# A convolution mixer's input projection: pairs of output tiles by seven half-size products, weight sums on GpSimd, some low weight parts by adding transfers

## The chip, the core and the metric

The kernel runs on one core of a Trainium2 chip. The core has a matrix engine (TensorE; PE in the profile, its weight loads PEld), a vector engine (VectorE, DVE), an activation engine (ScalarE, ACT), a general engine (GpSimd, POOL) and a queue engine that starts transfers (SyncE, SP), all with their own instruction streams that run in order and wait on semaphores. The metric is the device time of one execution in microseconds, median of the runs.

## The reference, cut to what matters

A trunk of four layers (mLSTM, short convolution, dilated attention, pooling) is run for 512 prompt tokens and 8 sample tokens that share all weights. The change is in layer 1:

```python
def shortconv_mixer(h, w_in, conv_w, w_out, buf):
    u = h @ w_in                       # 520 x 1024 by 1024 x 8192
    bg, cg, xb, z = jnp.split(u, 4, axis=-1)
    cx = cg * xb
    ...
    cpad = jnp.concatenate([buf.astype(cx.dtype), cx], axis=1)
    y = conv_w[0] * cpad[:, 0:T]
    for j in range(1, CONV_W):
        y = y + conv_w[j] * cpad[:, j:j + T]
    out = (bg * y * jax.nn.silu(z)) @ w_out
    return out, cpad[:, -(CONV_W - 1):]
```

All data are float32, and the products must come out at about float32 accuracy.

## The kernel before, in words

Activations lie with features on the 128 partitions and the 520 tokens along the free axis; a layer's input is 8 such tiles (1024 features). A weight tile is 128 x 1024: the 128 output features of one tile of the result, for 8 chunks of 128 input features. Every float32 operand is used as two float32r parts, hi = the rounded value and lo = the rest, and a product is hi·hi + hi·lo + lo·hi. `mm6` (L193) does this for one chunk: 3 products, each in two parts of 256 and 264 tokens, so 6 matmuls. `proj` (L213) makes one tile of the result from 8 chunks, 48 matmuls.

Weights come in the order that `plan` (L39) lists. `weights` (L181) is called when a tile is needed; it runs `cast` four tiles ahead and `fetch` six ahead: a load on SP (L165), the hi part by ACT (`wh`, L175) and the lo part by DVE (`wl`, L177, the load minus wh).

`conv` (L782) is layer 1's mixer. Its input projection has 64 weight tiles `w_b`. For each of 16 blocks j it takes four of them: 32+j (xb), 16+j (cg), j (bg) and 48+j (z). cx = cg·xb (L799), the taps of the convolution are one ACT instruction (L807) and four DVE ones (L810 to L813), POOL copies the last columns of cx out as state (L803, L804), and bg·y·silu(z) is made and split by `gated` (L517: L525, L528, L530) while the next block runs. `work` in `finish_norm` (L307) makes the normalised input tiles and their parts between the projections, from the `tick` that `proj` calls after every second chunk. The output projection `w_bo` follows (`out_proj`, L345). PSUM has two tiles of 1024 columns (`ps`) and four of 512 (`ax`).

Nothing moves instructions after the code has been written: each engine's order is the order of the calls.

Of the kernel before, what the change touches and what calls it, by code (L numbers as in the profile page):

```python
# [14 lines left out]
P = 128  # L15
# [8 lines left out]
H = 8  # L24
# [13 lines left out]

def plan():  # L39

    out = []

    def end(i, name, halves, begun=False):
        cs = range(2 if halves else 1)
        out.extend((name, j, c) if halves else (name, j) for c in cs for j in range(2) if c or not begun)
        out.extend((name, j, c) if halves else (name, j) for j in range(2, KD) for c in cs)
        for j in range(KD):
            if j % 4 == 0:
                out.append(("w_pe", i, j // 4))
# [12 lines left out]
    end(2, "w_co", False)
    for g in range(4):
        for n, (u, i) in enumerate(POOLED):
            if g and n == 2:
                out.extend(("w_grp", g - 1, i) for i in range(2))
            out.append(("w_d", 16 * u + 4 * g + i))
    out.extend(("w_do", j, 0) for j in range(2))
    out.extend(("w_grp", 3, i) for i in range(2))
    end(3, "w_do", True, True)  # L70
    return out

# [41 lines left out]
class Net:  # L114
    def __init__(self, ctx, tc, d):
# [5 lines left out]
        self.wp = pool("w", bufs=3)  # L121
# [7 lines left out]
        self.gate, self.finish = Gate(0.5), None  # L129
        self.wkeys, self.wf, self.wc = plan(), {}, {}  # L130
        self.wpos = self.ndma = self.ncast = 0
# [28 lines left out]

    def fetch(self, upto):
        while self.ndma < min(upto, len(self.wkeys)):
            key = self.wkeys[self.ndma]
            wf = self.wp.tile([P, 1024], F32, tag="wf", name=self.nm("wf"))
            self.nc.sync.dma_start(wf, self.d[key[0]][key[1:]])  # L165
            self.wf[self.ndma] = wf
            self.ndma += 1

    def cast(self, upto):
        nc = self.nc  # L170
        while self.ncast < min(upto, len(self.wkeys)):
            self.fetch(self.ncast + 1)
            wf = self.wf.pop(self.ncast)
            wh = self.wp.tile([P, 1024], F32R, tag="wh", name=self.nm("wh"), bufs=4)
            nc.scalar.activation(wh, wf, AF.Copy)  # L175
            wl = self.wp.tile([P, 1024], F32R, tag="wl", name=self.nm("wl"), bufs=4)
            nc.vector.tensor_sub(wl, wf, wh.bitcast(F32))  # L177
            self.wc[self.ncast] = (wh, wl)
            self.ncast += 1

    def weights(self, *key, ahead=4):  # L181
        i = self.wpos
        assert self.wkeys[i] == key, (self.wkeys[i], key)
        self.wpos += 1
        self.cast(i + ahead)
        self.fetch(i + 2 + ahead)
        return self.wc.pop(i)
# [5 lines left out]
    def mm6(self, ps, w, c, a, start, stop, m=P):  # L193
# [8 lines left out]
        for j in range(2):  # L202
            mm(out[j], wl, a[0][:, PARTS[j]], start=False, stop=stop)  # L203

# [8 lines left out]
    def proj(self, name, *idx, a):  # L213
# [5 lines left out]
        for c in range(0, n, 8):  # L219
            w = self.weights(name, *idx, *([c // 8] if n > 8 else []))  # L220
            for k in range(8):
                self.mm6(ps, w, k * P, a[c + k], c + k == 0, c + k == n - 1)
                if k % 2:
                    self.tick()
        return ps[:, BASE : BASE + T]

    def proj_pair(self, name, a, n):

        ps = self.psum(), self.psum()
        for c in range(0, n, 8):  # L230
            w = []
            for lo, hi in ((0, 7), (7, 8)) if c + 8 == n else ((0, 8),):
                for j in range(2):
                    if not lo:
                        w.append(self.weights(name, j, *([c // 8] if n > 8 else []), ahead=4 - j))
# [7 lines left out]
    def need(self, a, i):  # L243

        while len(a) <= i:
# [54 lines left out]
    def finish_norm(self, hs, g0, wait, idle, pace):  # L300
# [6 lines left out]
        def work():  # L307
# [14 lines left out]
            for _ in range(idle):  # L322
                yield
            new = []
# [18 lines left out]


    def out_proj(self, name, y, i, begun=None):  # L345
# [7 lines left out]
        for j in range(KD):  # L353
# [6 lines left out]
            xs.append(self.split(self.x[j]))  # L360
        return xs

    def embed(self, i, xs):
# [24 lines left out]
        self.finish_norm(hs, g0, 3, *((4, 4), (2, 3), (0, 0))[i])  # L388
# [393 lines left out]
    def conv(self, h, lay):  # L782
        nc, d, tc = self.nc, self.d, self.tc
        self.streams = [self.norm, self.gate]
        y = []
        ex = lay.enter_context(tc.tile_pool(name="cvy", bufs=16))
        with ExitStack() as st:
            mp = st.enter_context(tc.tile_pool(name="cv", bufs=1))
            sin = mp.tile([P, 16, 2, NS], F32, name="cv_in")
# [4 lines left out]
            for j in range(16):  # L794
# [8 lines left out]
                nc.gpsimd.tensor_copy(po[:, j], cx[:, NP - 2 : NP])  # L803
                nc.gpsimd.tensor_copy(so[:, j, 1], cx[:, NP:T])  # L804
                w0, w1, w2 = (self.col(C_CW + 16 * t + j) for t in range(3))
                yc = self.act()
                nc.scalar.activation(yc, cx, AF.Copy, scale=w2)  # L807
                ps = self.proj("w_b", j, a=h)
                stt = nc.vector.scalar_tensor_tensor
                stt(yc[:, 1:NP], cx[:, 0 : NP - 1], w1, yc[:, 1:NP], ALU.mult, ALU.add)  # L810
                stt(yc[:, 2:NP], cx[:, 0 : NP - 2], w0, yc[:, 2:NP], ALU.mult, ALU.add)
                stt(yc[:, NP:T], sin[:, j, 1], w1, yc[:, NP:T], ALU.mult, ALU.add)
                stt(yc[:, NP:T], sin[:, j, 0], w0, yc[:, NP:T], ALU.mult, ALU.add)  # L813
                nc.vector.tensor_mul(yc, self.ready(ps), yc)
# [524 lines left out]
```

## Time and profile before

| | us |
|---|---|
| median of 3 runs | 2192.8 |
| range of the runs | 2190.49 to 2194.71 |
| the profiled execution, its own time | 2191.75 |
| its span in the trace | 2190.0 |
| busy in the span: PE, DVE, ACT, POOL | 2170.4, 1336.6, 784.0, 226.8 |

A busy time is the union of an engine's instructions. Matmuls overlap in the pipeline, so one lasts some 285 ns by the trace and a new one starts about every 120 ns; what a matmul costs is read from a stretch of time and the matmuls in it. The convolution's input projection is the stretch from 606 to 975 us, its output projection the one from 975 to 1060 us.

### The profile page before, as it was taken

What the parts mean: (1) busy time and instruction counts of PE and PEld (TensorE: products, weight loads), DVE (VectorE), ACT (ScalarE), POOL (GpSimd) and SP (SyncE); (2) the same over time, 40 slices, a digit from 0 to 9 for tenths busy, and PEclk for the clock granted to TensorE, in tenths of its full rate; (3) what the DMA queues carried; (4) which work ended last, traced back from release to release, by engine and by line L of the source; (5) the groups of instructions that cost most, each with busy time, mean ns of one, the idle gap of its engine ahead of it and who ended that gap; (6) DMA issues with size and microseconds to landing.
All of it is one profiled execution on the core that took longest, in us unless ns stands there. A gap on an engine that the chain in (4) does not pass through costs nothing.

```text
span 2190.0 us, 42581 instructions
## 1 busy us (share of the span) xinstructions
PE 2170.4 (99%) x17788; PEld 2154.2 (98%) x17788; DVE 1336.6 (61%) x2984; ACT 784.0 (36%) x1286; POOL 226.8 (10%) x338
## 2 busy tenths in 40 slices
PE   9999999999999999999999999999999999999998
PEld 8999999999999999999999999999999999999998
DVE  7677676653575344333467877787777466676434
ACT  6444444432442222222333323333335343222233
POOL 1101110100000000000014232232220000000000
PEclk9999999999999999999999999999999999999999
DMA  4643544333232322233233645554545233323421
GB/s 151 203 163 139 184 168 150 98 97 97 90 97 87 97 89 95 92 105 95 83 103 127 187 168 179 172 181 155 184 161 194 87 106 97 97 88 97 124 88 51
DMA packets 104643, 275.17 MB, mean 126 GB/s; under 512 B 33316, under 2 KB 37668, under 8 KB 102404
## 3 DMA queue, kind: packets, MB, share of 16 engines
q1 hardware_dynamic: 104308, 272.41, 38.3%
q8 instruction: 139, 2.28, 0.4%
q14 instruction: 52, 0.43, 0.1%
q10 hardware_dynamic: 144, 0.06, 0.0%
HBM read 249.61 MB, written 22.82 MB: 124 GB/s over the span
## 4 chain that ended last, share of the span: by engine, by line
PE 91%; DVE 3%; ACT 1%; POOL 1%; issue 0%; DMA 0%; SPq 0%; POOLq 0%; DVEq 0%; ACTq 0%
PE ps L199 27%; PE ps L201 27%; PE ps L203 27%; PE ax L925 1%; PE ax L998 1%; PE ax L201 1%; PE ax L203 1%; PE ax L199 1%; PE ax L969 1%; PE ax L654 1%; PE ax L673 1%; DVE wl L177 1%; DVE a L329 0%; POOL a L877 0%; PE ax L936 0%
## 5 line engine op out<-in xcount | busy, mean ns | idle before, releaser
L199 PE MATMUL ps<-hi,wh 128*128 128x256 f32 (+1 forms) x5280 | 1086.3, 287 | 2.1 <-DVE a L278 1.6
L201 PE MATMUL ps<-lo,wh 128*128 128x256 f32 (+1 forms) x5280 | 1062.9, 283 | 0.1
L203 PE MATMUL ps<-hi,wl 128*128 128x256 f32 (+1 forms) x5280 | 1063.1, 283 | 0.0
L199 PEld LDWEIGHTS ps<-hi,wh 128*128 128x128 f32 x5280 | 822.3, 189 | 7.6 <-issue 2.5
L201 PEld LDWEIGHTS ps<-lo,wh 128*128 128x128 f32 x5280 | 819.3, 188 | 0.3 <-DVE lo L530 0.3
L203 PEld LDWEIGHTS ps<-hi,wl 128*128 128x128 f32 x5280 | 818.3, 188 | 0.0
L177 DVE TENSOR_TENSOR wl<-wf,wh 128x1024 fp32r<-128x1024 f32 x344 | 429.2, 1249 | 397.1 <-ACT wh L175 395.5
L175 ACT ACTIVATE wh<-wf 128x1024 fp32r<-128x1024 f32 x344 | 361.0, 1051 | 253.2 <-issue 201.7
L271 ACT ACTIVATE a<-ps 128x520 f32<-128x520 f32 x94 | 56.3, 599 | 247.7 <-PE ps L203 243.5
L876 POOL TENSOR_TENSOR a<-a,a 32x520 f32<-32x520 f32 x48 | 74.0, 1542 | 386.2 <-DVE a L278 199.6
L359 DVE TENSOR_TENSOR x<-ps,x 128x520 f32<-128x520 f32 x32 | 22.4, 699 | 103.4 <-PE ps L203 103.3
L278 DVE TENSOR_TENSOR a<-ps,a 128x520 f32<-128x520 f32 x95 | 65.9, 694 | 25.9 <-PE ps L203 22.5
L282 ACT ACTIVATE a<-a 128x520 f32<-128x520 f32 x43 | 27.5, 639 | 150.2 <-DVE a L278 150.0
L259 ACT ACTIVATE hi<-x 128x520 fp32r<-128x520 f32 x32 | 20.5, 639 | 164.6 <-DVE x L359 164.6
L877 POOL TENSOR_TENSOR a<-a,a 32x520 f32<-32x520 f32 x48 | 66.4, 1384 | 124.8 <-DVE a L875 88.7
L902 ACT ACTIVATE S<-S,nmx 128x128 f32<-128x128 f32 (+1 forms) x96 | 40.0, 417 | 76.1 <-DVE nmx L899 76.1
L252 DVE CUSTOM_DVE_ANT_0 kc<-kc,qb 128x128 f32<-128x128 f32 (+1 forms) x192 | 56.8, 350 | 12.5 <-DMA kc<-kc 12.5
L252 DVE CUSTOM_DVE_ANT_0 vc<-vc,pb 128x128 f32<-128x128 f32 (+1 forms) x192 | 61.6, 379 | 0.0
L880 DVE TENSOR_TENSOR a<-a,a 32x520 f32<-32x520 f32 x48 | 37.2, 776 | 17.3 <-POOL a L877 17.3
L260 DVE TENSOR_TENSOR lo<-a,hi 128x520 fp32r<-128x520 f32 x40 | 28.0, 699 | 31.3 <-ACT hi L259 31.3
L732 DVE SCALAR_TENSOR_TENSOR Ci<-kqb,wv,Ci 128x128 f32<-128x128 f32 x128 | 37.1, 346 | 12.2 <-DMA kqb<-scr_kq 10.1
L528 ACT ACTIVATE hi<-a 128x520 fp32r<-128x520 f32 x40 | 25.4, 635 | 50.6 <-DVE a L525 50.6
(272 smaller groups left out, 1759.7 us busy)
## 6 DMA issues: line engine op xcount, KB each, us to landing
wf<-w_c SPq DMA_DIRECT2D x80, 512.0 KB
wf<-w_a SPq DMA_DIRECT2D x64, 512.0 KB
wf<-w_b SPq DMA_DIRECT2D x64, 512.0 KB
wf<-w_pg SPq DMA_DIRECT2D x32, 512.0 KB
wf<-w_d SPq DMA_DIRECT2D x32, 512.0 KB
pb<-scr_p SPq DMA_DIRECT2D x8, 1292.0 KB
Ci<-C_in SPq DMA_DIRECT2D x16, 512.0 KB
kqb<-scr_kq SPq DMA_DIRECT2D x8, 1024.0 KB
```

Source lines behind the costliest of these rows:

```text
L175: nc.scalar.activation(wh, wf, AF.Copy)
L177: nc.vector.tensor_sub(wl, wf, wh.bitcast(F32))
L199: mm(out[j], wh, a[0][:, PARTS[j]], start=start, stop=False)
L201: mm(out[j], wh, a[1][:, PARTS[j]], start=False, stop=False)
L203: mm(out[j], wl, a[0][:, PARTS[j]], start=False, stop=stop)
L252: self.nc.vector.tensor_tensor_reduce(junk, a, b, 1.0, 0.0, ALU.mult, ALU.add, out)
L271: nc.scalar.activation(dst[:, :T], ps, func, scale=scale)
L278: nc.vector.tensor_mul(dst[:, :T], ps, self.r)
L876: nc.gpsimd.tensor_mul(b[:32], t[:32], cs[0])
L877: nc.gpsimd.tensor_mul(a[:32], a[:32], cs[1])
L880: nc.vector.tensor_add(t[:32], a[:32], b[:32])
L902: nc.scalar.activation(blk, blk, AF.Exp, bias=nmx[:, i : i + 1], scale=SCALE, accum_out=l[:, i : i + 1])
```

## The change

The first three blocks (NPLAIN) stay as they were. From block 3 on, the block's weight tiles are taken in two pairs, first (32+j, 16+j), then (j, 48+j), and each pair is one call of `seven`. It sees the product as two by two by two: two output tiles (w1, w2), two halves of the 1024 inputs (a, b: 512 columns of a weight tile each) and two halves of 260 tokens. Seven products of half size, in place of eight, make the two tiles. The weight operands are w1a, w1b, w2a' (in place: w1a − w2a), w2b and three sums s1, s2, s4. They are multiplied with input halves (11, 21, 22) and sums of those (T1 to T4). Each product is 4 chunks of 3 matmuls with 260 columns. The order on PE is: w1a·11, s2·T2, s1·T1, w1b·21, then the s4·22 of the pair before (`flush`), w2a'·T3, w2b·T4. After some of them ACT (L376, L384) or DVE (L379, L388, L392, and L371 behind the late product) add the results up.

The sums of weights are four GpSimd instructions a pair (L276 to L279), and the sums of the inputs 16 instructions of 260 columns, made once (`summed`). The parts hi and lo of s1, s2 and s4 are made by ACT and DVE (`hs`, `ls`, 512 columns). For the first tile of every w_b and w_bo item (the single tiles of blocks 0 to 2 and of w_bo too) the lo part is no longer a DVE subtraction: ACT writes −hi into it (L257), and a transfer that GpSimd issues adds the weight from memory onto it (L259). The two other parts of the work of a block are run when a pair's last product is there: `first` (cx and the taps) inside the second pair, `second` (silu and bg·y) inside the next block's first pair. The parts of y are made at the end, four of them in the last pair and the rest as the output projection asks for them.

When a step is written is now set by a list, `due`: it gives each load, split, sum and part a time on a clock in which a plain tile costs 5.76 and a pair 10.08, and `pump`, called after every matmul group, writes all that is due. Four loads can be held in place of three. The descriptor memory of GpSimd's transfers is set to 1024 bytes.

```diff
+NPLAIN = 3
+HALF = T // 2
+FBUFS, HBUFS, SBUFS = 4, 4, 4
+MOVED = ("w_b", "w_bo")
...
+        else:
+            ld, ld2 = sorted(slots["wf"])[:2]
+            one = at(max(ld, ld2, t - 12.8), i, "sum")
+            h1 = at(max(ld, take("wh", t + 5.76), t - 14.4), i, "high")
+            h2 = at(max(ld2, take("wh", t + 10.08), one + 4), i, "high2")
+            low1 = at(h1 + 1.3 if it.moved else max(h1 + 1.3, one + 3), i, "low")
+            low2 = at(max(h2 + 1.3, one + 3), i, "low2")
+            at(take("wf", max(low1, one + 5.8)) - 0.01, i, "load")
+            at(take("wf", low2) - 0.01, i, "load2")
+            for n, need, until in (("2", t - 7.2, t + 2.88), ("1", t - 5.7, t + 4.32), ("4", t - 1.4, t + 17.3)):
+                h = at(max(take("hs", until), need, one + 3), i, "high" + "s" + n)
+                at(h + 0.6, i, "lows" + n)
...
+        def high(k, tag, n=1024, pool=None):
+            t["h" + k] = new(tag, n, pool)
+            nc.scalar.activation(t["h" + k], t["w" + k], AF.Copy)
+
+        def low(k, tag, n=1024, pool=None):
+            t["l" + k] = new(tag, n, pool)
+            if k == "1" and it.moved:
+                nc.scalar.activation(t["l1"], f(t["h1"]), AF.Copy, scale=-1.0)
+                key = it.keys[0]
+                nc.gpsimd.dma_start(t["l1"], self.d[key[0]][key[1:]], accum_op=ALU.add)
+                return
+            nc.vector.tensor_sub(t["l" + k], t["w" + k], f(t["h" + k]))
...
+        elif op == "sum":
+            w1, w2 = t["w1"], t["w2"]
+            s1, s2, s4 = (self.act()[:, :512] for _ in range(3))
+            nc.gpsimd.tensor_add(s1, w2[:, a], w2[:, b])
+            sub(w2[:, a], w1[:, a], w2[:, a])
+            sub(s2, s1, w1[:, a])
+            sub(s4, w1[:, b], s2)
...
+    def seven(self, keys, B, dst, done):
...
+        def product(out, w, name, start):
+            for k in range(4):
+                c = slice(k * P, (k + 1) * P)
+                hi, lo = B[name][k]
+                go = {} if start else {"skip_group_check": True}
+                mm(out, w[0][:, c], hi, start=start and k == 0, stop=False, **go)
+                mm(out, w[0][:, c], lo, start=False, stop=False, **go)
+                mm(out, w[1][:, c], hi, start=False, stop=k == 3, **go)
...
+        def last():
+            product(r5, part("s4"), "22", False)
+            add(dst[0][:, HALF:], r5, u2)
+            done()
+            step()
+
+        product(r1, part("1", a), "11", True)
+        nc.scalar.activation(s1, r1, AF.Copy)
+        step()
+        product(r6, part("s2"), "T2", True)
+        add(u2, r6, s1)
+        step()
+        product(r5, part("s1"), "T1", True)
+        step()
+        product(r1, part("1", b), "21", False)
+        nc.scalar.activation(dst[0][:, :HALF], r1, AF.Copy)
+        step()
+        self.flush()
+        product(r6, part("2", a), "T3", False)
+        add(u3, r6, s1)
+        step()
+        product(r4, part("2", b), "T4", True)
...
+                def first():
+                    nc.vector.tensor_mul(cx, cx, xb)
+                    c.extend(taps(j, cx))
+                    conv(j, cx, *c)
+
+                def second():
+                    nc.scalar.activation(z, z, AF.Silu)
+                    nc.vector.tensor_mul(c[0], bg, c[0])
+                    self.gate.gens.append(times(c[0], z))
+
+                self.seven((("w_b", 32 + j), ("w_b", 16 + j)), self.sums, (xb, cx), first)
...
+                    self.seven((("w_b", j), ("w_b", 48 + j)), self.sums, (bg, z), second)
...
-    nc = bacc.Bacc("TRN2", target_bir_lowering=False, num_devices=1)
+    nc = bacc.Bacc("TRN2", target_bir_lowering=False, num_devices=1, dynamic_dma_scratch_size=1024)
```

On PE, before, one chunk of a w_b tile is six matmuls in two token parts (`wh` and `wl` are the weight's parts, `hi` and `lo` the input's, `ps` the result):

```order
L199 MATMUL ps_8930<-hi_7307,wh_8753 128x256
L199 MATMUL ps_8930<-hi_7307,wh_8753 128x264
L201 MATMUL ps_8930<-lo_7336,wh_8753 128x256
L201 MATMUL ps_8930<-lo_7336,wh_8753 128x264
L203 MATMUL ps_8930<-hi_7307,wl_8755 128x256
L203 MATMUL ps_8930<-hi_7307,wl_8755 128x264
```

Now, in a pair, a chunk of a product is three matmuls of 260 columns; here the end of w1a·11 and the beginning of s2·T2 (`ha`, `la` are the parts of the input sums T1 and T2, `hs`, `ls` those of a weight sum):

```order
L361 MATMUL ax_9466<-hi_7691,wh_9290 128x260
L362 MATMUL ax_9466<-lo_7707,wh_9290 128x260
L363 MATMUL ax_9466<-hi_7691,wl_9292 128x260
L361 MATMUL ax_9467<-ha_7339,hs_9385 128x260
L362 MATMUL ax_9467<-la_7341,hs_9385 128x260
L363 MATMUL ax_9467<-ha_7339,ls_9389 128x260
```

PE has 16,983 rows before and 16,671 now, 312 fewer: 12 for each of 26 pairs (84 matmuls in place of 96).

On POOL, before, there are two small copies of cx for each block and nothing else, here to the end of block 9:

```order
L804 COPY cv_s<-a_8746 128x8
L803 COPY cv_p<-a_8986 128x2
L804 COPY cv_s<-a_8986 128x8
L803 COPY cv_p<-a_9226 128x2
L804 COPY cv_s<-a_9226 128x8
```

Now, in the middle of the stage, POOL has for each pair an adding transfer and the four sums of the pair after; the transfer waits for ACT's −hi (`wl` is its target):

```order
L259 DMA wl_9425<-w_b 128x1024
L276 TENSOR_TENSOR a_9441<-wf_9247 128x512
L277 TENSOR_TENSOR wf_9247<-wf_9229,wf_9247 128x512
L278 TENSOR_TENSOR a_9442<-a_9441,wf_9229 128x512
L279 TENSOR_TENSOR a_9443<-wf_9229,a_9442 128x512
L1053 COPY cv_p<-a_9333 128x2
L1054 COPY cv_s<-a_9333 128x8
L259 DMA wl_9562<-w_b 128x1024
```

The transfer stands in the queue ahead of the next pair's sums, so these can't begin before it is issued.

On ACT, before, around a block's taps (L807), there is one split of a weight tile (L175) between two pieces of the block's own work:

```order
L271 ACTIVATE a_8928<-ps_8869 128x520
L175 ACTIVATE wh_8931<-wf_8817 128x1024
L807 ACTIVATE a_8990<-a_8986,cols 128x520
L175 ACTIVATE wh_8993<-wf_8874 128x1024
L175 ACTIVATE wh_9053<-wf_8935 128x1024
```

Now, in a block's second pair, from the first evacuation (L376) to that of the next pair:

```order
L376 ACTIVATE a_9469<-ax_9466 128x260
L252 ACTIVATE wh_9484<-wf_9247 128x1024
L252 ACTIVATE hs_9515<-a_9442 128x512
L384 ACTIVATE a_9335<-ax_9466 128x260
L252 ACTIVATE hs_9534<-a_9441 128x512
L1057 ACTIVATE a_9554<-a_9333,cols 128x520
L252 ACTIVATE wh_9560<-wf_9369 128x1024
L257 ACTIVATE wl_9562<-wh_9560 128x1024
L252 ACTIVATE hs_9598<-a_9443 128x512
L376 ACTIVATE a_9609<-ax_9606 128x260
```

The taps (L1057) now stand ahead of the split and the −hi that the next adding transfer waits for, and the −hi ahead of the evacuation that PE's fourth product waits for.

On DVE the same second pair now reads as follows (`ls` and `wl` are lo parts; L379, L371, L388 and L392 add PSUM results; L1095 is cx, L1062 to L1065 the taps):

```order
L261 TENSOR_TENSOR ls_9463<-a_9310,hs_9461 128x512
L1069 TENSOR_TENSOR a_9064<-a_9284,a_9064 128x520
L379 TENSOR_TENSOR a_9469<-ax_9467,a_9469 128x260
L261 TENSOR_TENSOR wl_9501<-wf_9247,wh_9484 128x1024
L261 TENSOR_TENSOR ls_9519<-a_9442,hs_9515 128x512
L261 TENSOR_TENSOR ls_9536<-a_9441,hs_9534 128x512
L371 TENSOR_TENSOR a_9332<-ps_9338,a_9339 128x260
L1095 TENSOR_TENSOR a_9333<-a_9333,a_9332 128x520
L1062 SCALAR_TENSOR_TENSOR a_9554<-a_9333,cols,a_9554 128x511
L1063 SCALAR_TENSOR_TENSOR a_9554<-a_9333,cols,a_9554 128x510
```

Before, the same place has one subtraction a weight tile and the block's own work:

```order
L525 TENSOR_TENSOR a_8867<-a_8750,a_8867 128x520
L177 TENSOR_TENSOR wl_8933<-wf_8817,wh_8931 128x1024
L530 TENSOR_TENSOR lo_8926<-a_8867,hi_8925 128x520
L799 TENSOR_TENSOR a_8986<-ps_8930,a_8928 128x520
L177 TENSOR_TENSOR wl_8995<-wf_8874,wh_8993 128x1024
L810 SCALAR_TENSOR_TENSOR a_8990<-a_8986,cols,a_8990 128x511
```

Cx (L1095) now stands behind three lo parts whose inputs come from POOL's sums by way of ACT.

## Rows read from the trace of the kernel before

**Rows 1.** The page: busy time of the engines, the granted clock of PE in 40 slices (tenths of full speed), and the chain that ended last.

```profile
PE 2170.4 (99%) x17788; PEld 2154.2 (98%) x17788; DVE 1336.6 (61%) x2984; ACT 784.0 (36%) x1286; POOL 226.8 (10%) x338
...
PEclk9999999999999999999999999999999999999999
...
PE 91%; DVE 3%; ACT 1%; POOL 1%; issue 0%; DMA 0%; SPq 0%; POOLq 0%; DVEq 0%; ACTq 0%
```

**Rows 2.** Busy time by stretch: the stretch, its length, then busy us (and instructions) of PE, PEld, DVE, ACT and POOL, PE's granted clock, the mean busy share of the 16 transfer engines, GB/s. The convolution's input projection, its output projection, and the stretch with the most transfers at the kernel's start.

```profile
606.00:975.00 369.00, 369.00 (x3079) 368.88 (x3078) 172.72 (x225) 110.39 (x137) 4.97 (x32) 1.00 0.30 94
975.00:1060.00 85.00, 84.83 (x708) 84.65 (x708) 29.56 (x33) 21.33 (x25) 0.00 (x0) 1.00 0.30 94
60.00:70.00 10.00, 10.00 (x85) 9.80 (x85) 3.69 (x9) 3.40 (x9) 0.00 (x0) 1.00 0.88 346
```

**Rows 3.** Groups of instructions of like shape in the input projection (610 to 975 us): busy us, mean ns of one, idle time before them and who ended it.

```profile
L177 DVE TENSOR_TENSOR wl<-wf,wh 128x1024 fp32r<-128x1024 f32 x64 | 78.4, 1225 | 152.1 <-ACT wh L175 152.1
L175 ACT ACTIVATE wh<-wf 128x1024 fp32r<-128x1024 f32 x64 | 67.2, 1050 | 40.8 <-issue 40.7
L810 DVE SCALAR_TENSOR_TENSOR a<-a,cols,a 128x511 f32<-128x511 f32 x16 | 11.9, 745 | 0.0
L807 ACT ACTIVATE a<-a,cols 128x520 f32<-128x520 f32 x16 | 11.7, 731 | 76.5 <-DVE a L799 76.5
L799 DVE TENSOR_TENSOR a<-a,a 128x520 f32<-128x520 f32 x3 | 2.1, 700 | 0.2
L803 POOL COPY cv_p<-a 128x2 f32<-128x2 f32 x16 | 2.9, 184 | 353.6 <-DVE a L799 353.6
```

**Rows 4.** Groups of like shape over the whole span, the nearest ones to the new instructions: a full-height GpSimd sum of 512 columns, DVE and ACT on some 260 columns from PSUM, ACT on 512 and 520 columns, the same columns as above.

```profile
L628 POOL TENSOR_TENSOR a<-a,a 128x512 f32<-128x512 f32 x8 | 10.4, 1304 | 18.4 <-DMA a<-scr_g 18.1 <-POOL os_all L500 0.3
L380 DVE TENSOR_TENSOR a<-ax,a 128x264 f32<-128x264 f32 x31 | 13.1, 423 | 0.0
L677 ACT ACTIVATE a<-ax 128x256 f32<-128x256 f32 x32 | 12.3, 384 | 62.5 <-DVE num L676 62.4
L975 ACT ACTIVATE a<-ax 128x512 f32<-128x512 f32 x16 | 9.5, 596 | 24.4 <-PE ax L969 23.2 <-issue 1.2
L282 ACT ACTIVATE a<-a 128x520 f32<-128x520 f32 x43 | 27.5, 639 | 150.2 <-DVE a L278 150.0
```

**Rows 5.** GpSimd and DVE side by side, in time order (start us, duration us): two GpSimd sums in a row and the DVE instructions beside them at 1215 us; then, in the order of the queries, a full-height GpSimd sum and the DVE subtraction beside it at 99 us.

```profile
1215.18 1.29 POOL L877 TENSOR_TENSOR a<-a,a 32x520 f32<-32x520 f32 x1 [6.12 <-DVE a L875]
1216.44 1.31 POOL L876 TENSOR_TENSOR a<-a,a 32x520 f32<-32x520 f32 x1
...
1215.02 0.66 DVE L971 COPY a<-ax 128x512 f32<-128x512 f32 x1
1216.51 1.80 DVE L880 TENSOR_TENSOR a<-a,a 32x520 f32<-32x520 f32 x1 [0.83 <-POOL a L877]
...
99.03 1.30 POOL L628 TENSOR_TENSOR a<-a,a 128x512 f32<-128x512 f32 x1
...
99.81 1.61 DVE L177 TENSOR_TENSOR wl<-wf,wh 128x1024 fp32r<-128x1024 f32 x1 [3.99 <-ACT wh L175]
```

**Rows 6.** The same two engines at 1401 us: a GpSimd sum that begins while DVE is busy with instructions of two inputs in SBUF.

```profile
1401.45 2.75 POOL L876 TENSOR_TENSOR a<-a,a 32x520 f32<-32x520 f32 x1 [5.32 <-ACT a L271]
...
1401.22 0.68 DVE L880 TENSOR_TENSOR a<-a,a 32x520 f32<-32x520 f32 x1
1401.83 1.21 DVE L177 TENSOR_TENSOR wl<-wf,wh 128x1024 fp32r<-128x1024 f32 x1
```

**Rows 7.** SP's issue of one weight load (start us, duration us), and a transfer of 512 KB in the chain that ended last (start us, us).

```profile
1133.95 0.33 SPq L165 DMA_DIRECT2D wf<-w_c  x1
...
1192.89 5.52 DMA kc<-kc
```

More of the change, by code (lines that the diff above doesn't have):

```diff
@@ new lines, in pump @@
+    def pump(self, step=0.0):
+        nxt = self.items[min(self.wpos, len(self.items) - 1)].begin
+        self.clock = max(self.clock, min(self.clock + step, nxt))
+        by = self.clock - 0.01 if step else self.clock + 0.01
+        while self.begun < len(self.ops) and self.ops[self.begun][0] <= by:
+            self.make(*self.ops[self.begun][2:])
+            self.begun += 1
+    def fetch(self, upto):
+        for i in range(upto):
+            self.make(i, "load")
+    def cast(self, upto):
+        for i in range(upto):
+            self.make(i, "load")
+            self.make(i, "split")
@@ L182, in weights, with item @@
+    def item(self, *keys):
         i = self.wpos
-        assert self.wkeys[i] == key, (self.wkeys[i], key)
+        assert self.items[i].keys == keys, (self.items[i].keys, keys)
         self.wpos += 1
-        self.cast(i + ahead)
-        self.fetch(i + 2 + ahead)
-        return self.wc.pop(i)
+        self.clock = self.items[i].begin
+        self.pump()
+        while any((j, op) not in self.made for _, _, j, op in self.ops[self.begun :] if j == i):
+            self.make(*self.ops[self.begun][2:])
+            self.begun += 1
+        return self.wt.pop(i)
@@ L234, in proj_pair @@
                     if not lo:
-                        w.append(self.weights(name, j, *([c // 8] if n > 8 else []), ahead=4 - j))
+                        w.append(self.weights(name, j, *([c // 8] if n > 8 else [])))
+                    if c == 0 and self.look:
+                        if j:
+                            for k in range(8):
+                                self.need(a, k)
+                                for m in range(2):
+                                    self.mm6(ps[m], w[m], k * P, a[k], k == 0, False)
+                                self.tick()
+                        continue
                     for k in range(lo, hi):
@@ L298, in square_in, with finish_norm @@
             nc.vector.tensor_add(self.acc, self.acc, sq)
-    def finish_norm(self, hs, g0, wait, idle, pace):
+    def finish_norm(self, hs, g0, wait, idle, pace, sums=None):
         nc = self.nc
@@ L323, in work @@
                 yield
+            if sums is not None:
+                hs[:] = yield from self.summed(g0, r, sums)
+                self.hraw = False
+                return
             new = []
@@ L811, in conv @@
[L811 to L814, printed above, removed]
[L815 to L816 removed]
+                c = taps(j, cx)
+                ps = self.proj("w_b", j, a=h)
@@ new lines, in parts @@
+            def parts(n):
+                hi = self.act(F32R, "hi", ex if n > 3 else None)
+                nc.scalar.activation(hi, yf[n], AF.Copy)
+                yield
+                lo = self.act(F32R, "lo")
+                nc.vector.tensor_sub(lo, yf[n], hi.bitcast(F32))
+                y.append((hi, lo))
+            for j in range(NPLAIN, 16):
+                block(j)
+            self.flush()
+            self.gate.drain()
+            while self.gate.run:
+                self.gate.step()
@@ L817, in conv @@
+            self.gate.gens.extend(parts(n) for n in range(4, 16))
+            self.look = 4
             nc.sync.dma_start(d["o_conv_p"], po)
```

250 lines of the change are left out of this document (203 added, 47 removed).

## The prediction

> **What bounds the kernel now.** I read the page first: PE is busy 99% of the span at the full granted clock (all 40 slices at 9 or more tenths, the 2.4 GHz level), and 91% of the chain that ended last is PE [rows 1]. Next the stretches: in the input projection of the convolution PE is busy for all of its 369.00 us, with 3079 matmuls, so one costs 369.00 / 3079 = 0.1198 us, while DVE is busy 172.72, ACT 110.39 and POOL 4.97 us [rows 2]. So time is won there only by fewer matmuls, and lost as soon as another engine is later than PE. Last the prices [rows 3, 4] and the instructions of GpSimd and DVE that stand side by side [rows 5, 6], since the change gives GpSimd work that it has not had.
>
> **What it removes.** 26 pairs by 12 matmuls are 312; at 0.1198 us that is 37.4 us, all on the path. A pair becomes 84 matmuls = 10.06 us, a block from the fourth on two of them, 20.13 us, a product 1.44 us. 260 columns are the mean of today's 256 and 264, so I take the price of one as unchanged.
>
> **What it adds, by engine and block** (20.13 us). ACT: per pair three instructions of 1024 columns (1.05), three of 512 (0.60), two of 260 from PSUM (0.38), per block the taps (0.73) and a silu (0.64): 12.8 us [rows 3, 4]. It fits. DVE: two subtractions of 1.23, six of 512 columns (0.69 at most, the row of 520 being 0.70), three products of two tiles (0.70), taps 1.9, and per pair three sums of 260 (0.42) and one of 520 (0.70) from PSUM: 14.5 us [rows 3, 4]. It fits too, alone. POOL: eight sums of 1.26 (the start-to-start time of two in a row [rows 5]), 10.1 us, two copies of 0.18 and two issues.
>
> DVE and POOL are not alone, however. Beside a GpSimd sum a DVE subtraction that normally takes 1.23 takes 1.61, and ends 1.09 after the sum does; one of 520 columns takes 1.80 and ends 0.56 after it; a copy from PSUM (0.66) is not held up [rows 5]. The other way round a GpSimd sum took 2.75, since two DVE instructions in a row came first, the second begun after it, and ended 1.16 after the second [rows 6]. So a GpSimd sum and a DVE instruction with two inputs in SBUF exclude each other, and DVE keeps its turn over instructions in a row. Together they need 8 x 1.26 + 2 x 1.09 + 6 x 0.56 + 3 x 0.56 + some 1.9 for the taps = 19.2 of 20.13 us. It fits by a hair, and only if nothing waits in line.
>
> **It does wait in line: the loop.** The adding transfer of a pair is issued by POOL behind ACT's −hi and ahead of the next sums; the sums feed ACT and DVE; and ACT comes to the next −hi behind these. I follow that loop through a block, with g for POOL's issue.
>
> Second pair of a block: g; three sums up to L278, 3.78; DVE's part of s4 and L1069 get in between, 2 x 0.56; then the lo part of w2, 1.09, that of s2, 0.56, L279, 1.2, that of s1, 0.56; L371 0.42 and L1095 0.70; on ACT the taps 0.73, the split 1.05 and −hi 1.05. Sum 12.26 + g.
>
> First pair of a block: g; three sums, 3.78, and one part between, 0.56; on ACT the hi part of s2 0.60, L384 0.38, hi of s1 0.60, silu 0.64, split and −hi 2.10. Sum 8.66 + g.
>
> Both are 20.92 + 2g, against 20.13 on PE. So the loop is longer than PE's block by 0.79 + 2g, and that is lost in each round once the slack is used. The slack is small: with no lag −hi of the second pair is done 11.14 us after the pair's start (product five ends at 7.19, then 0.42, 0.70, 0.73, 2.10), 1.08 into the next; hi of s4 and L376 end at 2.06; PE's fourth product, which adds onto what L376 reads, begins at 4.31. Slack 2.25 us. Thirteen blocks give twelve rounds.
>
> **The price g** stands in no row. Below: 0.33, an issue on SP [rows 7]. Above: 1.30, a whole GpSimd sum [rows 4]. I take 0.65, twice the row of like kind and half of the one of like engine; nothing suggests a gain. Then a round loses 2.09 us, twelve lose 25.1, less the slack 2.25: 22.8 us of stalls. By the ends: 0.33 gives 15, 1.30 gives 38. The Trainium skill gives a figure for a transfer issued from GpSimd (DMA: Bandwidth & Descriptors, Latency and other measured facts): a first byte after about 1 us, put down to the software that writes the descriptors; no run here shows it. By it a round would lose 2.8 us and all 31 us, an estimate, and the change would gain 6 us.
>
> **What costs nothing.** The adding transfers: a load a plain tile (48 x 0.1198 = 5.75 us) keeps the 16 engines busy 0.30 of the time [rows 2], so one is 1.73 us of them all, and three in 10.06 us are 0.52; were an adding one three times as dear, 0.86, and 0.88 has been reached [rows 2]. One issued 1.7 us into a pair is wanted at the pair after, 8.4 us later; a 512 KB transfer on the chain took 5.52 [rows 7]. If it took over 8.4, PE would wait for the rest in every pair. The 16 sums of the inputs (260 columns, half of 1.26 each, 10 us) lie beside 69 us of plain blocks. In w_bo the low parts go from DVE to ACT, which is busy 21.33 of 85 us [rows 2], and to transfers begun three tiles ahead. The other stages keep the order of their work but for loads that move by a few places: 0, give or take 1 us.
>
> **The sum.** 2191.75 − 37.4 + 22.8 = 2177.2 for the profiled execution; the median lies 1.05 above it (2192.8), so 2178.
>
> **Rivals.**
> 1. The loop hardly binds. If s4's parts and L1069 run before POOL gets to its sums, 3 x 0.56 fall out, the round loses 0.4 and the whole 3 us: 2158. For: DVE has 5.6 us of a block to itself. Against: by my sum both become ready at about the same time. At the least, no stall at all: 2155.
> 2. Gain and loss cancel. This is so with g from 1.07 to 1.44 (twelve rounds of 2.9 to 3.7 us): 2188 to 2197.
> 3. Slower: the issues on POOL have to take turns with DVE as the sums do. The GpSimd sum that met two DVE instructions in a row lost 2.75 − 1.30 = 1.45 us [rows 6]. One issue in a block stands beside the two taps L1062 and L1063, two instructions in a row, the other beside a part of s4 and L1069 (1.1). The round would lose 2.09 + 1.45 + 1.1 = 4.64, all twelve, less the slack, 53.4: 2209. It decides from the point where the two issues of a block take 2.5 us together, turns included. Against: a transfer's issue reads no tile. The Trainium skill speaks for it in part (SBUF — State Buffer, the warning on DVE blocking a transfer): while DVE holds the port it shares with GpSimd, GpSimd can't write the descriptors of its own transfers. It says so for DVE's two-port modes, and no run here shows it for the form used here.
>
> **How the numbers follow.** Forecast, the loop binds and part of the gain is left (2162 to 2188): 0.48. Rival 1 (under 2162): 0.24. Rival 2: 0.14. Rival 3 (over 2197, late transfers included): 0.14. A change of 0.2%, 4.4 us, is about what a measurement of this kernel tells from none; so faster 0.72, same 0.14, slower 0.14. The range goes from no stall, 2156, to 2198: it leaves out the upper part of rival 3 and the edge of rival 1.
>
> **What would show it.** The stretch of the input projection is read as 369.0 − 37.4 plus its stalls: PE's idle time there should be about 23 us, in waits of some 2 us once a block, in the first pair, by the fourth product on ACT's L376. DVE's 512-column parts and POOL's sums should last over 1 and 1.3 us in turn. PE not idle means that the loop is shorter than I reckon (rival 1). Waits on `wl` by PE mean late adding transfers. POOL's issue, not seen in the trace of before, gives g itself. Wrong altogether would be a matmul of 260 columns that costs more than 0.12 us, or stalls outside this stage.

## The result, and the profile after

The changed kernel takes 2216.4 us (median of 4 runs, 2215.77 to 2216.89) beside 2192.15 for the kernel before: ratio 1.0109, 95% interval 1.0093 to 1.0125. It is 24 us slower, above the end of the range. The profiled execution took 2216.13, with a span of 2214.4.

Three lines of its page (engines; costliest groups; DMA issues):

```profile
PE 2149.8 (97%) x17476; PEld 2122.8 (96%) x17476; DVE 1451.1 (66%) x3116; ACT 893.9 (40%) x1466; POOL 463.6 (21%) x512
...
L259 POOL DMA_DIRECT2D wl<-w_b x38 | 33.9, 892 | 281.4 <-ACT wl L257 277.9
...
wl<-w_b POOLq DMA_DIRECT2D x38, 512.0 KB, 5.6
```

Beside [rows 1]: 312 matmuls are gone (17788 before, 17476 now), as said, but PE is busy 97% of a longer span, not 99%. GpSimd's busy time has doubled. An issue of an adding transfer lasts 0.89 us, and its data are there 5.6 us later.

Where the time went is read off one tile that every layer touches, the ones (`onesd`) of the norm's sum. The view of that tile from 600 to 1200 us has the norms that end layers 0 and 1, as first and last start. The kernel before:

```profile
L313 PE MATMUL ax<-a,onesd x8: 377/382/387, 608.4 to 1128.1; 128*128 128x256 f32 x4, 128*128 128x264 f32 x4
```

The changed kernel:

```profile
L519 PE MATMUL ax<-a,onesd x8: 379/382/386, 630.1 to 1153.2; 128*128 128x256 f32 x4, 128*128 128x264 f32 x4
```

Layer 0, the mLSTM stage, which has no pair in it, ends 21.7 us later. The convolution's layer took 523.1 in place of 519.7, though 37.4 us of matmuls are gone from it: 41 us of new stalls. The layers behind give back about 1 us.

What PE waited for, over the whole span (us in total, times, longest):

```profile
PE ax L361 <- ACT a L376: 16.3, 12, 1.4
PE ax L929 <- DVE C L917: 11.2, 5, 3.6
PE ps L333 <- DVE a L484: 7.8, 5, 2.0
PE ax L361 <- DVE a L379: 7.5, 11, 0.7
...
PE ps L361 <- DVE a L392: 2.7, 1, 2.7
```

The first is the wait that the prediction named: eleven of the twelve, 1.4 us each, stand in the first pairs of the third to the thirteenth block of pairs, and the twelfth (1.15 us) in the last pair. The second stands in the mLSTM stage. The eleven for L379 stand in second pairs; the prediction had none there.

**The loop, as GpSimd shows it** (start us, duration us, idle before and what ended it), for one block of the changed kernel:

```profile
835.91 0.89 POOL L259 DMA_DIRECT2D wl<-w_b  x1 [2.83 <-ACT wl L257]
836.53 1.59 POOL L276 TENSOR_TENSOR a<-wf 128x512 f32<-128x512 f32 x1
838.20 1.63 POOL L277 TENSOR_TENSOR wf<-wf,wf 128x512 f32<-128x512 f32 x1
839.79 1.29 POOL L278 TENSOR_TENSOR a<-a,wf 128x512 f32<-128x512 f32 x1
841.16 2.18 POOL L279 TENSOR_TENSOR a<-wf,a 128x512 f32<-128x512 f32 x1
845.52 0.90 POOL L259 DMA_DIRECT2D wl<-w_b  x1 [2.18 <-ACT wl L257]
...
858.81 0.90 POOL L259 DMA_DIRECT2D wl<-w_b  x1 [2.83 <-ACT wl L257]
```

From issue to issue 9.61 and 13.29 us: GpSimd waits for ACT's −hi each time, as the loop says. A block lasts 22.90, against 20.13 on PE. The −hi ahead of the second issue ends at 845.11, 0.41 us before the issue begins:

```profile
844.05 1.06 ACT L257 ACTIVATE wl<-wh 128x1024 fp32r<-128x1024 f32 x1
```

**The mLSTM stage, as SP shows it.** The queue of SP in the middle of one head, from the store of the states (o_C_s) to the broadcast read kqb. The kernel before:

```profile
175.44 0.34 SPq L736 DMA_DIRECT2D o_C_s<-Ci  x1
175.89 0.37 SPq L165 DMA_DIRECT2D wf<-w_a  x1
176.35 1.26 SPq L606 DMA_DIRECT2D a<-scr_g  x2
184.14 0.33 SPq L165 DMA_DIRECT2D wf<-w_a  x1
184.53 0.90 SPq L709 DMA_DIRECT2D Ci<-C_in  x2
189.43 0.29 SPq L718 DMA_DIRECT2D scr_kq<-kqt  x1
190.74 0.33 SPq L720 DMA_DIRECT2D kqb<-scr_kq  x1
```

The changed kernel, the same head:

```profile
180.62 0.34 SPq L992 DMA_DIRECT2D o_C_s<-Ci  x1
189.32 4.24 SPq L269 DMA_DIRECT2D wf<-w_a  x2
193.64 0.86 SPq L862 DMA_DIRECT2D a<-scr_g  x2
194.55 0.90 SPq L965 DMA_DIRECT2D Ci<-C_in  x2
195.55 0.65 SPq L974 DMA_DIRECT2D scr_kq<-kqt  x1
202.60 0.33 SPq L976 DMA_DIRECT2D kqb<-scr_kq  x1
```

Two loads now stand together ahead of the reads, and both wait on SP until a buffer is free (8.3 and 3.5 us); the reads stand behind them. From the store on, scr_g is read after 13.0 us, not 0.9, and the states after 13.9, not 9.1. The write scr_kq then follows right behind the two loads of states, and kqb, which has to wait for it to land, is issued 7.05 us after it, not 1.31. So kqb comes 22.0 us after the store, not 15.3. SP and DVE waited, from 100 to 480 us in the changed kernel:

```profile
SPq L269 <- DVE wl L261: 164.9, 28, 8.4
...
SPq L976 <- DMA scr_kq<-kqt: 39.6, 7, 6.8
...
DVE Ci L988 <- DMA kqb<-scr_kq: 46.6, 7, 8.8
```

In the kernel before the same three are:

```profile
SPq L165 <- DVE wl L177: 103.0, 24, 6.8
...
SPq L720 <- DMA scr_kq<-kqt: 6.2, 7, 1.0
...
DVE Ci L732 <- DMA kqb<-scr_kq: 10.1, 6, 2.0
```

DVE stands at L988 with the eviction L917 behind it, and PE's L929 waits for that; in the head shown above:

```profile
207.47 1.14 DVE L988 SCALAR_TENSOR_TENSOR Ci<-kqb,wv,Ci 128x128 f32<-128x128 f32 x4 [8.78 <-DMA kqb<-scr_kq]
...
210.75 1.68 PE L929 MATMUL ax<-vtok,a 128*128 128x257 f32 x4 [3.62 <-DVE C L917]
```

The clock adds to it. PE's matmuls and granted clock in three stretches around the wait of 3.62 us at 210.7 (us, then busy and count of each engine; PEclk):

```profile
208.00:212.00 4.00, 1.25 (x4) 0.89 (x5) 3.91 (x10) 0.00 (x0) 1.25 (x2) 0.94 0.12 31
212.00:216.00 4.00, 4.00 (x19) 3.64 (x19) 3.02 (x15) 0.95 (x4) 0.00 (x0) 0.64 0.69 268
216.00:220.00 4.00, 4.00 (x31) 3.86 (x30) 3.06 (x12) 1.91 (x5) 0.43 (x1) 1.00 0.00 0
```

Behind the wait the mean clock is 0.64 of full, so part of those 4 us ran at the 1.2 GHz level, and 19 matmuls were done where 31 follow at full clock. Up to the norm that ends the stage, PE's waits add up to 20.8 us where the kernel before has 7.3, and in four stretches of 10 us (from 100, 210, 300 and 350 us) the mean granted clock is 0.83 where it was 1.00. That is 13.5 and 4 x 10 x 0.17 = 6.8, together 20.3 of the 21.7 us.

### The profile page after: what moved, and what is told of

It reads as the page before. It is cut to its first block, busy times and chain, and to the rows that moved or that the text cites. A ratio compares the mean times of both kernels' runs of the same rounds, so it can differ in the third digit from the quotient of the medians.

```text
span 2214.4 us, 42595 instructions
## 1 busy us (share of the span) xinstructions
PE 2149.8 (97%) x17476; PEld 2122.8 (96%) x17476; DVE 1451.1 (66%) x3116; ACT 893.9 (40%) x1466; POOL 463.6 (21%) x512
## 3 DMA queue, kind: packets, MB, share of 16 engines
q1 hardware_dynamic: 104308, 272.41, 37.4%
## 4 chain that ended last, share of the span: by engine, by line
PE 68%; DVE 10%; issue 3%; ACT 3%; POOL 3%; DMA 2%; DVEq 0%; SPq 0%; ACTq 0%; POOLq 0%
PE ps L333 19%; PE ps L335 19%; PE ps L337 19%; DVE ls L261 3%; ACT wh L252 2%; PE ax L1241 1%; PE ax L1314 1%; PE ax L335 1%; PE ax L337 1%; PE ax L333 1%; DVE wl L261 1%; DMA scr_kq<-kqt 1%; POOL wf L277 1%; DVE a L1069 1%; POOL a L276 1%
## 5 line engine op out<-in xcount | busy, mean ns | idle before, releaser
L333 PE MATMUL ps<-hi,wh 128*128 128x256 f32 x4448 | 920.1, 288 | 8.2 <-DVE a L484 7.8
L335 PE MATMUL ps<-lo,wh 128*128 128x256 f32 x4448 | 895.4, 283 | 0.2 <-DVE lo L786 0.2
L337 PE MATMUL ps<-hi,wl 128*128 128x256 f32 x4448 | 894.7, 282 | 0.8 <-DMA wl<-w_bo 0.8
L333 PEld LDWEIGHTS ps<-hi,wh 128*128 128x128 f32 x4448 | 694.6, 189 | 14.6 <-issue 7.5
L337 PEld LDWEIGHTS ps<-hi,wl 128*128 128x128 f32 x4448 | 690.0, 189 | 1.0 <-DMA wl<-w_bo 1.0
L335 PEld LDWEIGHTS ps<-lo,wh 128*128 128x128 f32 x4448 | 690.2, 189 | 0.6 <-DVE lo L786 0.4
L261 DVE TENSOR_TENSOR wl<-wf,wh 128x1024 fp32r<-128x1024 f32 x290 | 366.8, 1268 | 203.7 <-ACT wh L252 201.6
L261 DVE TENSOR_TENSOR ls<-a,hs 128x512 fp32r<-128x512 f32 x78 | 111.2, 1450 | 1.0 <-ACT hs L252 1.0
L259 POOL DMA_DIRECT2D wl<-w_b x38 | 33.9, 892 | 281.4 <-ACT wl L257 277.9
L484 DVE TENSOR_TENSOR a<-ps,a 128x520 f32<-128x520 f32 x91 | 63.1, 694 | 21.3 <-PE ps L337 17.9
L361 PE MATMUL ax<-hi,wh 128*128 128x260 f32 x208 | 59.9, 288 | 16.3 <-ACT a L376 16.3
L988 DVE SCALAR_TENSOR_TENSOR Ci<-kqb,wv,Ci 128x128 f32<-128x128 f32 x128 | 38.2, 354 | 47.2 <-DMA kqb<-scr_kq 47.2
```

The costliest lines, as they stand in the source:

```text
L261: nc.vector.tensor_sub(t["l" + k], t["w" + k], f(t["h" + k]))
L333: mm(out[j], wh, a[0][:, PARTS[j]], start=start, stop=False)
L335: mm(out[j], wh, a[1][:, PARTS[j]], start=False, stop=False)
L361: mm(out, w[0][:, c], hi, start=start and k == 0, stop=False, **go)
L484: nc.vector.tensor_mul(dst[:, :T], ps, self.r)
```

## The experiments

The theory was that there are two separate losses, one by SP's order in the mLSTM stage, one by the sums on GpSimd in the convolution (the loop, and turns with DVE: a DVE instruction with two inputs in SBUF and a GpSimd sum do not run at once). Rivals: the adding transfers, the traffic of loads that start earlier, DVE's own load. All ratios are to the kernel before.

**1. SP's order of the mLSTM loads as before**, all else as changed:

```diff
+        if it.keys[0][0] == "w_a":
+            sp = at(begins[max(i - 3, 0)], i, "split")
...
+            at(min(begins[max(i - 5, 0)] + 0.005, sp - 0.01 if i < 4 else t), i, "load")
```

> The changed kernel, with one edit: in the mLSTM stage the weight loads stand in SP's queue where they stood before the change, with the four buffers kept. Theory A (order of SP's queue: a weight load that has to wait for a free buffer stands ahead of the state transfers, and DVE, ACT and then PE wait for these): the norm after the stage falls back from 630 to about 608 us, the whole from 2216 to about 2195 us, and PE's waits in that stage go. Rival B (four loads in flight crowd the transfer engines, whatever the order): the stage keeps 15 us or more of its loss. The convolution stage is as long as in the changed kernel, 522 us from norm to norm, by both.

Measured 2197.9, ratio 1.0029 (1.0016 to 1.0042): 18.5 us back.

**2. The planner alone**: all blocks plain, the code of the convolution and its norm's pace as before, no adding transfers; of the diff:

```diff
-NPLAIN = 3
+NPLAIN = 16
-MOVED = ("w_b", "w_bo")
+MOVED = ()
```

> The kernel before, with the new list of due times and the four load buffers, but no pairs, no adding transfers and the old order of the convolution. Theory A: the mLSTM stage alone is slower, by 21 to 22 us, the whole 2214 us. If the list of due times cost nothing there and the loss came from something that the pairs or the GpSimd transfers bring (descriptor memory, another stage), it would be 2192 us.

Measured 2210.9, ratio 1.0084 (1.0069 to 1.0099): 18.8 us lost with no pair in the program, and its SP waits 169.7 us in 29 waits on the low part that frees a buffer. The two runs agree from both sides.

**3. and 4. The sums of weights earlier**, with the new order of loads and with the old:

```diff
-            one = at(max(ld, ld2, t - 12.8), i, "sum")
+            one = at(max(ld, ld2, t - 18.0), i, "sum")
```

> The changed kernel, with one number: a pair's sums are due 18.0 ahead of it instead of 12.8, so in GpSimd's queue the sums of a pair now stand ahead of that pair's adding transfer and a whole step of the loop earlier. Nothing is taken from any engine. Theory A (the loop: -hi, issue, sums, parts, cx, taps, -hi): a block falls from 22.9 to 20.1 to 20.9 us, the convolution stage from 522 to 490 to 500 us, the whole to 2184 to 2194. Rival B (GpSimd and DVE exclude each other, and their turns alone are longer than PE's block): a block stays at 22 us or more, the whole at 2205 or more.

> Both edits, the old place of the loads in the mLSTM stage and the sums first. If both theories A hold and the two stages don't touch each other: 2216 less 22 less 22 to 32, that is 2162 to 2172, faster than the kernel before by 20 to 30 us. If the pairs are bound by the turns of GpSimd and DVE: 2184 or more.

Measured 2212.6 (1.0095, 1.0078 to 1.0112) and 2192.1 (1.0, 0.999 to 1.0009). The waits for L376 are gone but for one of 0.2 us, so the loop is open; yet only 4 to 6 us came back, far less than the 22 to 32 expected: the rival of both expectations, the turns, is what came true. What was late next, in run 4, over the pairs (PE's waits) and over two blocks (the stretch: us, busy of PE, PEld, DVE, ACT, POOL; then groups of instructions):

```profile
PE ax L369 <- DVE a L387: 16.2, 22, 0.9
...
754.50:798.70 44.20, 41.31 (x336) 40.49 (x336) 41.91 (x47) 23.92 (x37) 30.31 (x25) 1.00 0.60 144
...
L269 DVE TENSOR_TENSOR ls<-a,hs 128x512 fp32r<-128x512 f32 x13 | 16.0, 1256 | 0.0
L286 POOL TENSOR_TENSOR a<-a,wf 128x512 f32<-128x512 f32 x5 | 10.3, 2066 | 0.0
L269 DVE TENSOR_TENSOR wl<-wf,wh 128x1024 fp32r<-128x1024 f32 x4 | 9.2, 2307 | 0.0
L285 POOL TENSOR_TENSOR wf<-wf,wf 128x512 f32<-128x512 f32 x4 | 6.5, 1631 | 0.3
L1109 DVE TENSOR_TENSOR a<-a,a 128x520 f32<-128x520 f32 x2 | 3.6, 1810 | 0.1
```

A block lasts 22.10 us, and DVE is busy 41.91 of 44.20. It isn't working all of that time: a part of 512 columns lasts 1.26, one of 1024 2.31, a product 1.8. With the durations that the same instructions have in run 6, where GpSimd makes no sums, they would need 29.8 us; the other 12.1 are standing in turn behind GpSimd's sums.

**5. The sums of weights on DVE**, on top of run 4, and **6. the sums of the inputs too**:

```diff
-        sub = nc.gpsimd.tensor_sub
+        sub = nc.vector.tensor_sub
...
-            nc.gpsimd.tensor_add(s1, w2[:, a], w2[:, b])
+            nc.vector.tensor_add(s1, w2[:, a], w2[:, b])
```

> With both the sums of weights earlier and the loads in their old order, a block lasts 22.12 us, PE waits 16.2 us of the span for DVE's L379 addition, and DVE is busy 20.9 us of each block, its turns with GpSimd within. Here the eight sums of weights of a block are made by DVE (0.69 each at most) and none by GpSimd. Theory A, the turns between GpSimd and DVE are the bound: a GpSimd sum takes 1.6 us of the shared turn, the same sum on DVE 0.69, so the shared work of a block falls from some 22 to at most 20.1 us, the block to 20.2 to 20.6, and the time from 2192 to 2167 to 2174. Rival B, DVE is late because of its own order and load, whoever makes the sums: DVE gets 5.5 us more in a block, and the time stays or rises, 2192 to 2225.

> As the run before, and the 16 sums of the inputs in the plain blocks are made by DVE too. Theory A: the four waits of PE ahead of the pairs (1.49, 1.29, 1.62 and 3.10 us, for DVE's eviction that is late behind a subtraction that has to take turns) go in the main, 4 to 7 us less than the run before: 2161 to 2169. Rival B: those waits come from DVE's order, and they stay or grow by DVE's 16 x 0.42 us: 0 to 5 us more than the run before.

Measured 2167.1 (0.9873, 0.9858 to 0.9888) and 2161.6 (0.9857, 0.9842 to 0.9871), both as the theory of turns said; the 5.6 us between the two medians are no more than the two intervals leave open. DVE has eight sums more in a block and is less busy (41.2 us in 45 in run 6, 41.9 in 44.2 in run 4). The stretch of the pairs in run 6, all 262 us, and three groups of two of its blocks:

```profile
677.00:939.00 262.00, 260.24 (x2173) 260.03 (x2172) 231.55 (x390) 156.24 (x235) 26.94 (x53) 1.00 0.63 157
...
L269 DVE TENSOR_TENSOR ls<-a,hs 128x512 fp32r<-128x512 f32 x15 | 10.0, 685 | 0.1
L269 DVE TENSOR_TENSOR wl<-wf,wh 128x1024 fp32r<-128x1024 f32 x4 | 4.9, 1218 | 0.0
L284 DVE TENSOR_TENSOR a<-wf 128x512 f32<-128x512 f32 x4 | 2.7, 681 | 0.0
```

PE is idle for 1.8 of the 262 us, and no wait is listed there; DVE is busy 88% of the stretch, the same part costs 0.685 us in place of 1.256, and a sum 0.68 on DVE.

**7. Half of the second low part by an adding transfer too**, on top of run 6:

```diff
+            if k == "2":
+                nc.scalar.activation(t["l2"][:, b], f(t["h2"])[:, b], AF.Copy, scale=-1.0)
+                nc.gpsimd.dma_start(t["l2"][:, b], self.d[key[0]][key[1:]][:, b], accum_op=ALU.add)
+                nc.vector.tensor_sub(t["l2"][:, a], t["w2"][:, a], f(t["h2"])[:, a])
```

> As the run before, and in each pair half of the second tile's low part (512 columns) is made by -hi on ACT and an adding transfer in place of DVE: DVE has 2 x 0.54 us less in a block, GpSimd two issues of 0.9 us more, ACT 2 x 0.6 more. If DVE is still the bound of the block in the run before (over 20.2 us), the block falls by up to 1.1 us and the time by up to 13 us, to 2155 to 2160, some 37 below the kernel before at best. If PE is the bound already, or if GpSimd's issues hold something up, the time stays or rises by up to 10 us.

Measured 2160.7 (0.985, 0.9834 to 0.9867), no different from run 6: PE is the bound of the pairs already.

**8. No adding transfers in the input projection**, on top of run 4:

```diff
-MOVED = ("w_b", "w_bo")
+MOVED = ("w_bo",)
```

> Sums earlier and loads in their old order (2192), but the low part of the first tile of every pair (and of the plain tiles of blocks 0 to 2) is made by DVE again and no transfer adds to it; in the output projection the adding transfers stay. Theory A: DVE gets 2 x 2.3 us more in a block, turns with GpSimd included, and lasts some 26 us: 13 blocks x 4 = 50 us slower, 2230 to 2250. Rival C, what costs is the adding transfers themselves (the issue on GpSimd ahead of the sums, or their reading of memory): the loop through GpSimd's issue is gone, and the time falls below 2192, to 2165 to 2185.

Measured 2203.6 (1.0043, 1.0026 to 1.006): 9 us more than run 4 by the ratios, 11 by the medians. The sign rules out that the transfers are what costs; the size was a fourth of what I expected. Two blocks, in the columns of above:

```profile
753.00:799.50 46.50, 41.31 (x336) 40.49 (x336) 44.21 (x51) 20.35 (x33) 26.12 (x20) 1.00 0.31 91
```

A block is 23.25 us. I had priced each added low part at the 2.31 that it lasted beside the sums; but a wait in turn is not work that comes with the instruction. Reckoned as work without waits (durations of run 6), DVE's two-input instructions of a block of run 4 take 6 x 0.685 + 2 x 1.22 + 3 x 0.70 + 1.95 for the taps = 10.6 us, eight GpSimd sums at 1.30 [rows 4] 10.4: 21.0 of 22.1. Here it is 2 x 1.22 more, 23.4, beside 23.25. This reckoning was made after the runs; the 1.1 us that it leaves open in run 4 stay open.

**9. The changed kernel with all sums on DVE**, nothing else (the diff of run 5, and the same for the sums of the inputs):

> The changed kernel as it is (loads in the new order, sums at their first due times), but all sums, of the weights and of the inputs, made by DVE. The changed kernel took 2216.4: 21.7 us of it are lost in the mLSTM stage and some 37 to 40 given back in the convolution's. Theory A (the sums on GpSimd, by their turns with DVE and by the loop through its issue, cost all that the convolution gives back): the sums lie off GpSimd, so an issue no longer stands between sums; about 30 us come back and the mLSTM stage's 21.7 stay lost: 2180 to 2188. If the loop through -hi, GpSimd's issue and the taps were the cause without the turns, a third of it at most would come back: 2200 to 2212.

Measured 2183.6 (0.9961, 0.9946 to 0.9976): 32.8 us back by that alone, as the theory said, and no PE wait for L376 or L379 is left. The layer of the convolution falls from 523.1 to 488.6, the mLSTM stage keeps its loss (its norm comes at 633.1).

**10. The changed kernel with a fifth buffer for loads**; the order on every queue stays:

```diff
-            t[f"w{n}"] = self.wp.tile([P, 1024], F32, tag="wf", name=self.nm("wf"), bufs=FBUFS)
+            t[f"w{n}"] = self.wp.tile([P, 1024], F32, tag="wf", name=self.nm("wf"), bufs=FBUFS + 1)
```

> The changed kernel as it is, but with five buffers for loads in place of four; the order on every queue stays. In the mLSTM stage SP waits 165 us, 28 times, for the low part that frees a buffer, ahead of a load, and the reads of scr_kq, of the states and of the gates stand behind it in SP's queue. Theory A: with a buffer more the wait of a load starts one tile (5.76 us) later, nearly all 5.9 us of a wait go, and 12 to 20 of the 21.7 us come back: 2196 to 2204. Rival: what costs is the traffic of the loads that now start earlier, beside the reads; then the time stays at 2214 to 2220.

Measured 2197.3 (1.002, 1.001 to 1.0029): 19.1 us back, all of it in layer 0. Its norm tile and SP's wait for scr_kq:

```profile
L519 PE MATMUL ax<-a,onesd x8: 378/382/386, 608.2 to 1132.5; 128*128 128x256 f32 x4, 128*128 128x264 f32 x4
...
SPq L976 <- DMA scr_kq<-kqt: 14.2, 7, 3.5
```

The loads start even earlier here, and layer 0 is as short as before, so the rival (their traffic) falls; the wait on SP ahead of the reads was the cause.

**11. Run 6 with the sums at their first due time** (12.8, not 18.0):

> All sums on DVE, loads in the old order, but the sums of weights at their first due time (12.8 us ahead of the pair, not 18.0). If the loop through GpSimd's issue needs GpSimd's sums, the earlier time buys nothing now: 2158 to 2166, as with 18.0 (2161.6). If lateness of the sums alone costs, PE waits 1 to 2 us a block for L384, and the time is 2175 to 2190.

Measured 2163.7 (0.9868, 0.9853 to 0.9883), not to be told from run 6. With no sum on GpSimd there is no loop to open.

**12. Pairs from the third block on**, on top of run 7 (NPLAIN = 2):

> The quickest kernel so far (2160.7: all sums on DVE, half of the second low part by an adding transfer), with pairs from the third block on, not the fourth: 24 matmuls less, 2.9 us. The 16 sums of the inputs and their parts have to fit beside two plain blocks, 46 us, in place of three. If they fit: 2157 to 2159. If not, PE waits at the first pair for the parts of the inputs, up to some 15 us: 2160 to 2175.

Measured 2170.2 (0.99, 0.9885 to 0.9914), some 10 us worse than run 7, though 2.9 us of matmuls are gone. The parts of the inputs don't fit beside two plain blocks, and PE waits at the first pair for 4.6 us. Then the granted clock is at its lower level (0.50) from 658 to 666 us, and 30 matmuls are done there in 8 us beside 34 in the 4 us that follow, another 4 us; what else is lost stays open:

```profile
PE ax L376 <- ACT hi L590: 3.0, 1, 3.0
...
PE ax L377 <- DVE lo L594: 1.6, 1, 1.6
...
658.00:666.00 8.00, 7.36 (x30) 6.76 (x31) 6.54 (x12) 3.95 (x7) 0.88 (x1) 0.50 0.20 50
666.00:670.00 4.00, 4.00 (x34) 4.00 (x33) 2.63 (x5) 2.55 (x4) 0.00 (x0) 0.94 0.45 96
```

Runs 6 and 7 are quicker than both kernels, than the one before by some 32 and 33 us.

## Why the prediction was wrong

**Removed: right.** 312 matmuls are gone, and one of 260 columns costs what was taken: 260.24 us / 2173 = 0.1198 in run 6.

**"The other stages keep the order of their work but for loads that move by a few places: 0, give or take 1 us": the step that failed.** The forecast is missed by 38 us: 21.7 here, and 18 by stalls in the convolution (41 for 22.8), of which below; about 1 us came back behind. Without this step the time would have been 2197.9, but still 0.3% slower than before (run 1), so that the forecast of a gain failed by the sizes below as well. The instructions of the four engines do keep their order there, but for a split of a weight that moves by a place; SP's do not, and I looked at how far a load moves, not at what stands behind it once it has to wait for a buffer. Runs 1, 2 and 10 show it in three ways: the old order gives 18.5 us back, the new order alone loses 18.8, a fifth buffer gives 19.1 back. That the write of scr_kq lands late because the loads of states go just ahead of it is read from the times, not tried by itself.

**The loop: right in its place, mis-sized.** A round was to lose 2.09 us and loses 2.77. The slack was about right: the first of the twelve rounds shows no wait for L376. The other eleven lose 30.5 us where 22.8 were forecast for all. The legs were 8.66 + g and 12.26 + g, and measured 9.61 and 13.29, so g came out at 0.95 and 1.03 where 0.65 was taken. The issue itself holds the next sum back by 0.62 (836.53 − 835.91), near what was taken for it. What had been left out is the 0.41 us from the end of −hi on ACT to the beginning of the issue (845.11 to 845.52), about the same in every round. Most sums last 1.6 us, which with the turns between them is 0.1 to 0.2 us a leg more than reckoned, and the steps on ACT and DVE are quicker by about as much. PE is idle for 30.7 us of the stretch from 630 to 998 us, where about 23 had been named as the sign. The Trainium skill's figure for a first byte on this path (DMA: Bandwidth & Descriptors, Latency and other measured facts), about 1 us, gave 2.8 us a round. The round agrees with that, but the two spans measured here are other ones than a first byte, so the agreement may be luck.

**"It fits by a hair" (19.2 of 20.13): wrong.** With the loop open a block still lasts 22.1 (run 4). The turns were counted as eight sums and DVE's lags behind them, which leaves out most of DVE's own time in turn: by the reckoning under run 8 it is 21.0, and 22.1 were measured. The Trainium skill has the rule (SBUF — State Buffer, Who interferes with whom): a DVE instruction with two inputs in SBUF contends with a GpSimd one that reads SBUF. The trace agrees, with 1.256 us beside the sums and 0.685 without for the same part.

**"The 16 sums of the inputs lie beside 69 us of plain blocks": wrong by some 4 us.** PE waits three times for L484 there, 4.2 us in all. In the traces of runs 5 and 6, with these sums on GpSimd and on DVE, the same waits are 5.9 and 2.3 us and the layer is 494.9 and 491.4 us, so a part of the waits comes from the turns.

**Adding transfers cost nothing: right, their issue in the loop aside.** They land in 5.6 us, PE waits for one once, 0.8 us, in the output projection, and without them in the input projection it is slower (run 8).

**The rivals.** None was it. The third had the right neighbours, turns with DVE, but put them on the issues; they are on the sums. An issue lasts 0.89 us in the changed kernel and 0.87 in run 6, where no GpSimd sum stands beside it, so no turn was added to it. That the kernel came out slower, as this rival said, is luck. The part "stalls outside this stage" among what would make it wrong came true, without a price or a place.

The account of 2216.1 − 2191.75 = 24.4 us: −37.4 for matmuls; +21.7 in the mLSTM stage; in the convolution's layer +41 (11 x 2.77 = 30.5 in rounds, 4.2 in the plain blocks, 3.8 in the last pair, 0.8 for an adding transfer, the last 1.5 not traced to a wait); about −1 behind it.

## What to carry to other kernels

GpSimd gave DVE no relief here, where both read SBUF and DVE's instructions have two inputs there. Count the work of both as one engine's; the sums are then cheaper on DVE (0.69 for 1.30 us). The Trainium skill says as much (Perfetto Trace Analysis, Optimizing Scalar/DVE Operations): moving work between these two might not help; here moving it back gave 32.8 us. When a planner reorders loads, read for each queue what stands behind a load that has to wait for its buffer, in every stage and not only in the one that is changed; a spare buffer may be all that it needs.

## What was not expected of the hardware

PE's mean granted clock in the 4 us behind its waits in the mLSTM stage was 0.64 after one of 3.6 us, 0.62 after one of 2.0 (at 302.7) and 0.64 after one of 2.6 (349.8), but 1.00 after one of 2.3 (257.7); in the pairs, with a wait of 1.4 us and one of 0.7 in each 22.9, it stayed at 1.00. GpSimd starts its next sum 0.62 us after the start of an issue that lasts 0.89. Between the end of an ACT instruction and the issue on GpSimd that waits for it lay 0.41 us (845.11 to 845.52), while a GpSimd copy began 0.06 after the DVE instruction that it waits for (855.60 to 855.66). For a small write right behind two loads on the same queue SP waited 5.7 us in the mean and 6.8 at most (39.6 us in 7 waits), and 0.9 in the mean where the loads had gone some 5 us ahead. Why a GpSimd sum lasts 1.3 us in one place and 1.6 in another, where DVE holds it up by no whole instruction, stays open.
